# The reciprocal behind the mask: signed factors on the sums of a nested attention kernel

## The chip, the cores and the metric

The kernel runs on one core of a Trainium2 chip. The metric is the time of one execution on the device, in microseconds. The engines' names are those of the profile: PE is the tensor engine (PEld its weight loads), DVE the vector engine, ACT the scalar engine, POOL GpSimd, SP the engine that issues the DMAs.

## What is computed

Self-attention over 32 sequences of different lengths (between 64 and 511 rows of 512 numbers), with 8 heads of 64 and one weight matrix for queries, keys and values. Rows behind a sequence's end are zero in the output.

```python
for b in range(batch):
    x_b = x[b, :lengths[b]]
    q, k, v = np.split(np.matmul(x_b, w_qkv), 3, axis=-1)      # then split into heads
    scores = scale * np.matmul(q, k.transpose(0, 2, 1))
    attn = np.exp(scores - scores_max)
    attn = attn / (np.sum(attn, axis=-1, keepdims=True) + 1e-08)
    output[b, :lengths[b]] = np.matmul(attn, v)                # heads side by side
```

## The kernel before

The kernel first sorts the sequences by length on the chip, longest first, and then works on them in pairs: one round of a loop is two sequences, called the first and the second position (j is 0 and 1). There are twelve loops, one for each width in `LOOPS` (512, 448, then 384 down to 96 in steps of 32); a sequence of N rows is n tiles of 128 rows. For these lengths the rounds are: 512 one, 448 one, 384 one, 352 three, 320 one, 288 one, 256 one, 224 two, 192, 160, 128 and 96 one each. Loops of 4 tiles are 512 and 448; of 3 tiles 384 to 288; of 2 tiles 256 to 160; of 1 tile 128 and 96.

While the scores, exponentials and value products of one sequence run, PE also makes queries, keys and values of the next: its order within a position is written out by hand in `ORDER` (L238), step by step, with the PSUM banks of each step. "S" are scores, "A" value products, "B" queries and keys, "U" values there; "P" makes the next mask on DVE and lets POOL cast the next input; "X" transposes it by DMA; "L" writes the live rows' ones. What is ready for whom is kept by counting semaphores that `plan_waits` (L41) derives: an operation waits for the last writer or reader of each bank and tile it needs. A wait compares a semaphore with a register that grows from round to round.

The values tile `v_aug` has 65 columns a head: 64 values, and one column that is 1 for live keys and 0 for dead ones. So the value product over a bank gives, for each head and query tile, 64 sums and in column 64 (`HD`) the sum of the weights. Three DVE operations then make the output of a bank's heads, one set for each bank (`normed`, L1701) or for two neighbouring banks (`both_normed`, L1663):

- R (L1706, L1671): reciprocal of column 64, from PSUM into a small tile `rcp` of 4, 6 or 8 numbers a row.
- U (L1712, L1680): `rcp` times the ones and zeros of the live query rows, so that dead rows come out as zero. These are read from column 64 of `v_aug`, or, in the loops whose last tile is at most half full ("shared": 448, 320, 288, 192, 160), from a small tile `queries`, which `live_queries` (L1169) fills.
- O (L1715, L1693): the 64 sums of each head times `rcp`, from PSUM into the output tile `out_nat`. When O is done, PE may write the bank again, and SP may store the tile.

The loops of one tile have forms of their own (L1725 for a single bank), which fold the live rows into O.

Ahead of the loops stand the sort, the first casts and transposes and the whole projection of the first sequence. Each semaphore is given a start, its lead (L1905 on): the greatest distance, in positions, over which anyone waits for it. At L2048 these leads are put on by the owning engine (those of DVE by SP) before its first work. The list of operations of that head, in order, is `before_loops` (L382).

Of the kernel before, what the change touches and what calls it, by code (L numbers as in the profile page):

```python
# [18 lines left out]
P = 128  # L19
# [5 lines left out]
class Op:  # L25
# [12 lines left out]
    passed: object = None  # L38


def plan_waits(head, bodies, entries, rare):  # L41
# [22 lines left out]
    def follow(chain):  # L64
# [5 lines left out]
        for at, v in enumerate(chain):  # L70
# [10 lines left out]
            for w, j, k, op in todo:  # L81
# [17 lines left out]
                for wait in waits[w, j, k]:  # L99
                    got = [  # L100
                        o
                        for o in seen[wait[1]]
                        if wait[0] in ("last", "entry", "head", "lead")
                        or (wait[0] == "pos" and o["b"] == b - wait[2])
                        or (wait[0] == "iter" and o["b"] // 2 == b // 2 - wait[2])
                        or (wait[0] == "posin" and o["b"] == first - wait[2])
                        or (wait[0] == "posold" and older and o["b"] == first - wait[2])
                        or (wait[0] == "iterin" and o["b"] // 2 == first // 2 - wait[2])
                    ]
                    if got:  # L110
                        learn(got[-1])
# [7 lines left out]
                for o in sorted(needs, key=lambda o: -o["order"]):  # L119
# [23 lines left out]
                    else:  # L143
                        wait = ("pos", o["name"], b - o["b"])
# [8 lines left out]
                after = dict(mine)  # L153
# [9 lines left out]
                for r in op.writes:  # L163
                    write[r] = o
                    readers[r] = []
# [11 lines left out]
def kernel(  # L177
# [25 lines left out]
    def ring(n, shape, dtype, name, pool=const):  # L203
# [178 lines left out]
    def before_loops():  # L382
# [505 lines left out]
        )  # L888
        computed = small(
# [138 lines left out]
    def position(N, j, at, ring):  # L1028
# [140 lines left out]
        def live_queries():  # L1169
# [3 lines left out]
                scalar1=0.0,  # L1173
                scalar2=None,
                op0=ALU.add,
# [360 lines left out]
        def used_by(blocks, late=False):  # L1536
            if packed:
                mine = [todo.index(block) for block in blocks]
                mine = {min(k, len(todo) - 1) // across for b in mine for k in (b, b + 1)}
# [59 lines left out]
        def paired(p):  # L1599
# [7 lines left out]
                banks[k][:, 0 : heads * n * (HD + 1)].rearrange("p (g t d) -> p g t d", t=n, d=HD + 1)  # L1607
# [54 lines left out]

        def both_normed(both, ks):  # L1663

            k0, k1 = ks
            apart = both[1] - both[0]
            sums_ = psum[:, k0 : k1 + 1, 0 : heads * n * (HD + 1)]
            r = r_bufs[k0][:, 0 : 2 * heads * n]

            def reciprocal():  # L1670
                return nc.vector.reciprocal(  # L1671
                    out=r.rearrange("p (z g) -> p z g", z=2),
                    in_=sums_.rearrange("p z (g d) -> p z g d", d=HD + 1)[:, :, :, HD],
                )

            def only_live():
                rows = queries[:, 1 - j, 0:n] if half_last else v_aug[:, 0:n, both[0], HD]
                rows = rows.unsqueeze(1).broadcast_to([P, 2 * heads, n])
                each = r.rearrange("p (g t) -> p g t", t=n)
                return nc.vector.tensor_tensor(out=each, in0=each, in1=rows, op=ALU.mult)  # L1680

            def divide():
                to = o_t[:, 0:n, :].rearrange("p t (h d) -> p h t d", d=HD)
                if heads == 1:
                    to = to[:, both[0] : both[1] + 1 : apart]
                    got = sums_.rearrange("p z (t d) -> p z t d", d=HD + 1)[:, :, :, 0:HD]
                    by = r.rearrange("p (z t) -> p z t", t=n).unsqueeze(3).broadcast_to([P, 2, n, HD])
                else:
                    to = to[:, both[0] : both[1] + heads].rearrange("p (z g) t d -> p z g t d", z=2)
# [477 lines left out]
```

## Time and profile before

| | |
|---|---|
| median of 3 runs | 329.05 us (328.48 to 329.23) |
| profiled execution: first to last instruction | 328.5 us; the page has no other time of it |
| mean granted clock of PE | 0.994 |
| DMA | 68.85 MB, mean 210 GB/s |
| DVE waiting for PE, largest group (L1367) | 44.8 us in 39 waits |
| POOL waiting for DVE's masks (L1052) | 174.9 us in 28 waits |

A line of a group names the source line, the engine, the operation, the tiles as out<-in, the shapes as partitions x elements with their types, and the count; then busy us, mean ns of one, and the idle time of the engine ahead of them with what ended it. A row of the timeline gives the start and length in us; a stretch of equal instructions is one row, and square brackets hold the idle time before it. The chain is followed back from the last instruction to what released each step.

### The profile page before, as it was taken

Reading aid. Unit: us, or ns where it says so; the run is one execution under the profiler, and the core shown is the slowest. Engines: PE = TensorE matmul, PEld = TensorE weight load, DVE = VectorE, ACT = ScalarE, POOL = GpSimd, SP = SyncE. Lnnn points to the kernel's source line nnn. Section 1 sums busy time; section 2 is a strip of 40 time slices with the busy share of each in tenths; the row PEclk is TensorE's granted clock in tenths of the full one; section 3 lists DMA queues with packets and bytes.
Section 4 is the critical chain, followed back from the end, with each engine's and each line's share of the span. In section 5 each row is a group of like instructions: output and inputs, shape, how many; then the busy total and the mean of one; then the engine's idle time right before and its main releaser. Section 6 shows DMA issues by size and latency. Waiting matters only on the chain.

```text
span 328.5 us, 13310 instructions
## 1 busy us (share of the span) xinstructions
PE 311.6 (95%) x5092; PEld 202.3 (62%) x5092; DVE 197.7 (60%) x635; ACT 262.6 (80%) x413; POOL 101.9 (31%) x148
## 2 busy tenths in 40 slices
PE   6899999999999999999999999999998999999980
PEld 4444645555655556556656657667777886777860
DVE  6777567566666646456455465545575565776853
ACT  4379999897878988988978989899867779687761
POOL 6448040324030330330231243043222224435320
PEclk9999999999999999999999999999999999999997
DMA  6984749395858999696676766857459857966651
GB/s 217 382 278 80 251 140 327 76 354 153 304 52 298 224 269 258 197 268 224 233 214 224 255 194 205 211 174 242 156 131 227 183 176 164 223 206 177 193 180 66
DMA packets 69449, 68.85 MB, mean 210 GB/s; under 512 B 40720, under 2 KB 40720, under 8 KB 69392
## 3 DMA queue, kind: packets, MB, share of 16 engines
q1 hardware_dynamic: 69344, 68.12, 71.4%
q8 instruction: 33, 0.54, 0.7%
q14 instruction: 24, 0.20, 0.2%
q10 hardware_dynamic: 48, 0.00, 0.0%
HBM read 25.17 MB, written 33.55 MB: 179 GB/s over the span
## 4 chain that ended last, share of the span: by engine, by line
PE 84%; DVE 5%; DMA 3%; issue 2%; ACT 2%; SPq 1%; POOL 1%; DVEq 0%; POOLq 0%; ACTq 0%
PE banks L1323 41%; PE banks L1269 13%; PE banks L1517 12%; PE banks L300 6%; PE banks L311 6%; PE banks L1631 2%; DMA xT<-x 2%; DMA x_nat<-in_x_dram 2%; PE banks L1210 1%; PE banks L1557 1%; DVE out_nat L1715 1%; DVE rcp L1712 1%; DVE out_nat L1693 1%; SPq L328 1%; ACT et L1287 1%
## 5 line engine op out<-in xcount | busy, mean ns | idle before, releaser
L1287 ACT ACTIVATE et<-banks 128x704 f16<-128x704 f32 (+8 forms) x256 | 198.8, 825 | 27.8 <-PE banks L1269 24.7
L371 POOL TENSOR_TENSOR x<-x_nat,mask 128x512 f16<-128x512 f32 x83 | 84.2, 1041 | 184.3 <-DVE mask L1052 174.9
L1323 PE MATMUL banks<-xT,w_r 64*128 64x352 f16 (+9 forms) x1536 | 127.8, 294 | 1.8 <-DMA xT<-x 1.2
L1323 PEld LDWEIGHTS banks<-xT,w_r 64*128 64x128 f16 x1536 | 68.7, 94 | 39.0 <-PE banks L1323 8.5
L1269 PE MATMUL banks<-qz,kT 64*128 64x352 f16 (+11 forms) x624 | 77.5, 294 | 2.6 <-issue 0.7
L1715 DVE TENSOR_TENSOR out_nat<-banks,rcp 128x256 f32<-128x256 f32 (+1 forms) x110 | 53.0, 482 | 3.8
L1367 DVE CAST qz<-banks 128x448 f16<-128x448 f32 (+6 forms) x47 | 26.4, 561 | 45.2 <-PE banks L1323 44.8
L1517 PEld LDWEIGHTS banks<-v_aug,et 128*128 128x128 f16 x1240 | 41.7, 97 | 13.5 <-issue 6.8
L1517 PE MATMUL banks<-v_aug,et 128*128 128x65 f16 x1240 | 47.1, 194 | 0.0
L1323 PE MATMUL banks<-w_r,xT 64*128 64x512 f16 (+1 forms) x368 | 46.6, 372 | 0.3 <-ACT v_aug L1489 0.3
L1269 PEld LDWEIGHTS banks<-qz,kT 64*128 64x128 f16 x624 | 28.1, 93 | 25.9 <-issue 7.1
L1706 DVE RECIPROCAL rcp<-banks 128x4 f32<-128x4 f32 (+1 forms) x112 | 20.3, 181 | 20.7 <-PE banks L1517 7.3
L311 PE MATMUL banks<-w_r,xT 128*128 128x512 f16 x104 | 26.9, 381 | 0.5 <-DVE xT L782 0.5
L1386 DVE CAST v_aug<-banks 128x512 f16<-128x512 f32 x25 | 16.6, 690 | 17.9 <-PE banks L1323 17.9
L1323 PEld LDWEIGHTS banks<-w_r,xT 64*128 64x128 f16 x368 | 17.2, 94 | 14.1 <-PE banks L1323 1.0
L1367 ACT CAST kT<-banks 128x352 f16<-128x352 f32 (+6 forms) x47 | 22.5, 479 | 1.5 <-PE banks L1323 1.5
L300 PE MATMUL banks<-xT,w_r 128*128 128x160 f16 (+3 forms) x256 | 23.0, 243 | 0.5 <-DVE v_aug L1489 0.5
L1367 DVE CAST kT<-banks 128x352 f16<-128x352 f32 (+5 forms) x33 | 17.9, 552 | 7.7 <-PE banks L1323 7.6
L300 PEld LDWEIGHTS banks<-xT,w_r 128*128 128x128 f16 x256 | 16.6, 98 | 5.2 <-DMA xT<-x 0.6
L1367 ACT CAST qz<-banks 128x352 f16<-128x352 f32 (+6 forms) x33 | 15.3, 465 | 3.7 <-PE banks L1323 3.6
L1489 ACT CAST v_aug<-banks 128x512 f16<-128x512 f32 x15 | 8.8, 589 | 9.5 <-PE banks L311 9.5
L1631 PE MATMUL banks<-v_aug,et 64*128 64x65 f16 x624 | 14.2, 190 | 0.6 <-issue 0.6
(116 smaller groups left out, 193.3 us busy)
## 6 DMA issues: line engine op xcount, KB each, us to landing
x_nat<-in_x_dram SPq DMA_DIRECT2D x12, 768.0 KB, 6.4
out_dram<-out_nat SPq DMA_DIRECT2D x12, 768.0 KB, 4.0
x_nat<-in_x_dram SPq DMA_DIRECT2D x14, 512.0 KB, 4.5
out_dram<-zeros SPq DMA_DIRECT2D x12, 512.0 KB, 3.6
out_dram<-out_nat SPq DMA_DIRECT2D x12, 512.0 KB, 4.7
out_dram<-out_nat SPq DMA_DIRECT2D x4, 1024.0 KB, 7.0
x_nat<-in_x_dram SPq DMA_DIRECT2D x3, 1024.0 KB, 5.3
out_dram<-zeros SPq DMA_DIRECT2D x4, 768.0 KB, 4.7
```

Of the source, the lines that this page charges most:

```text
L300: last = nc.tensor.matmul(dst[:, 0:N], w_r[:, c, w0 : w0 + P], xT[:, c, 0:N], start=(c == 0), stop=(c == NC - 1),)
L311: last = nc.tensor.matmul(pv, xT[:, c, t * P : (t + 1) * P], w_r[:, c, 2 * D : 3 * D], start=(c == 0), stop=(c == NC - 1),)
L371: return engine.tensor_tensor(out=x16, in0=x32, in1=live.broadcast_to([P, D]), op=ALU.mult)
L1269: last = nc.tensor.matmul(psc[par][:, x * wide : x * wide + N], kT[r, i, c0 : c0 + P], qz[r, i, 0:N], start=True, stop=True,)
L1287: return nc.scalar.activation(out=et[:, :, x0:x1, 0:N], in_=got.rearrange("p j (x q) -> p j x q", q=wide)[:, :, x0:x1, 0:N], func=AF.Exp, ...
L1323: last = nc.tensor.matmul(to, lhs(rows, c), rhs(rows, c), start=(c == 0 and opens), stop=(c == NC - 1 and not opens),)
L1367: return lambda copy, bank: copy(out=buf[:, ms, 0:M], in_=bank[:, 0 : gm * M].rearrange("p (m q) -> p m q", q=M),)
L1386: return lambda copy, bank: copy(out=v_bufs[o][:, t, :, 0:HD], in_=bank.rearrange("p (h d) -> p h d", d=HD))
L1517: last = nc.tensor.matmul(pav[:, g, qt, :], e_bufs[e][:, c0 + qt * P : c0 + (qt + 1) * P], v_aug[:, kt, h, :], start=(kt == 0 and not (hal ...
L1631: last = nc.tensor.matmul(pavs[own][:, g, qt, :], e_bufs[e][rows, c0 + qt * P : c0 + (qt + 1) * P], (v_bufs[0] if ending else v_aug)[rows, ...
L1706: return nc.vector.reciprocal(out=rcp, in_=pav[:, :, :, HD])
L1715: return nc.vector.tensor_tensor(out=o_t[:, 0:n, h0 * HD : (h0 + heads) * HD].rearrange("p t (g d) -> p g t d", d=HD), in0=pav[:, :, :, 0:HD],
```

## The change

In the loops of 2 to 4 tiles the live query rows become factors of +1 (live) and -1 (dead). U now comes first: it multiplies the sums in column 64, read from PSUM, by these factors, into `rcp`. R then takes the reciprocal of `rcp` in place. O is max(rcp, 0) times the 64 sums, as one SCALAR_TENSOR_TENSOR: a dead row's negative reciprocal becomes 0. `queries` now holds the factors in all these loops: a new operation in the head fills it for the first sequence, and step "L" of the second position refills it where it did not before. A bank's sums lie by query tile and then head ("t g d") instead of head and then tile. O over two neighbouring banks is two instructions, one for each bank. The three copies into `queries` at the entries of the loops 448, 320 and 192 go.

The diff also brings in hooks whose tables are empty (`BACKS`, `LATE`), rewraps the text of `ORDER` without changing a step, and sets the leads of all operations that aren't DMAs or among five rare ones to one common number.

```diff
+        op(
+            "queries",
+            "DVE",
+            lambda: dve.tensor_scalar(
+                out=queries[:, 1, :], in0=alive[:, 0, :], scalar1=2.0, scalar2=-1.0, op0=ALU.mult, op1=ALU.add
+            ),
...
                 in0=alive[:, bass.ds(at("DVE") + j, 2), 0:n],
-                scalar1=0.0,
-                scalar2=None,
-                op0=ALU.add,
+                scalar1=2.0,
+                scalar2=-1.0,
+                op0=ALU.mult,
+                op1=ALU.add,
...
             pav = banks[k][:, 0 : heads * n * (HD + 1)].rearrange(
-                "p (g t d) -> p g t d", t=n, d=HD + 1
+                "p (t g d) -> p g t d", t=n, d=HD + 1
...
+        def parted(h0, sums_, r):
+
+            by = r.rearrange("p (t g) -> p t g", t=n).unsqueeze(3).broadcast_to([P, n, heads, HD])
+            return nc.vector.scalar_tensor_tensor(
+                out=o_t[:, 0:n, h0 * HD : (h0 + heads) * HD].rearrange("p t (g d) -> p t g d", d=HD),
+                in0=by,
+                scalar=0.0,
+                in1=sums_.rearrange("p (t g d) -> p t g d", t=n, d=HD + 1)[:, :, :, 0:HD],
+                op0=ALU.max,
+                op1=ALU.mult,
+            )
...
             def divide():
+                if n > 1:
+                    for z in range(2):
+                        last = parted(both[z], sums_[:, z], each[:, z])
+                    return last
...
             def reciprocal():
-                return nc.vector.reciprocal(out=rcp, in_=pav[:, :, :, HD])
+                return nc.vector.reciprocal(out=r, in_=total if n == 1 else r)
 
             def only_live():
-                rows = v_aug[:, 0:n, h0 : h0 + heads, HD].rearrange("p t g -> p g t")
-                if half_last:
-                    rows = queries[:, 1 - j, 0:n].unsqueeze(1).broadcast_to([P, heads, n])
-                return nc.vector.tensor_tensor(out=rcp, in0=rcp, in1=rows, op=ALU.mult)
...
+                rows = queries[:, 1 - j, 0:n].unsqueeze(2).broadcast_to([P, n, heads])
                 return nc.vector.tensor_tensor(
...
+                    out=r.rearrange("p (t g) -> p t g", t=n),
+                    in0=total.rearrange("p (t g) -> p t g", t=n),
+                    in1=rows,
                     op=ALU.mult,
                 )
...
-            whose = f"queries{j}" if half_last else f"vl{j}"
-            op(f"U{h0}", "DVE", only_live, (f"r{k}", whose), (f"r{k}",))
-            op(f"O{h0}", "DVE", divide, (f"bk{k}", f"r{k}"), (f"o{j}.{h0}",))
+            op(f"U{h0}", "DVE", only_live, (f"bk{k}", f"queries{j}"), (f"r{k}",))
+            op(f"R{h0}", "DVE", reciprocal, (f"r{k}",), (f"r{k}",))
+            op(f"O{h0}", "DVE", lambda: parted(h0, sums_, r), (f"bk{k}", f"r{k}"), (f"o{j}.{h0}",))
...
+            elif kind == "L" and not half_last and j:
+                op(
+                    "L",
+                    "DVE",
+                    lambda: (live_queries(), live(alive, 0, n))[1],
+                    (),
+                    (f"vl{o}", "queries0", "queries1"),
+                )
...
-                nc.vector.tensor_copy(out=queries[:, 1, 0:n], in_=v_bufs[0][:, 0:n, 0, HD])
...
+    alike = [name for name in lead if name not in by_dma | rare and lead[name]]
+    for name in alike:
+        lead[name] = max(lead[k] for k in alike)
```

Three places on DVE, with buffer numbers and waits. The first is the first position of loop 512, where the banks of the last two heads' products (`a7` and `a6`, on PE) are turned into output; `rcp_88` is the small tile of bank 3, `out_nat_77` the output tile. Before:

```order
L1706 RECIPROCAL rcp_88<-banks 128x4 [waits done_a7]
L1712 TENSOR_TENSOR rcp_88<-rcp_88,v_aug_67 128x4 [waits done_R7]
L1715 TENSOR_TENSOR out_nat_77<-banks,rcp_88 128x4x64 [waits done_ST0,done_U7]
L1706 RECIPROCAL rcp_87<-banks 128x4 [waits done_a6]
L1712 TENSOR_TENSOR rcp_87<-rcp_87,v_aug_67 128x4 [waits done_R6]
L1715 TENSOR_TENSOR out_nat_77<-banks,rcp_87 128x4x64 [waits done_U6]
```

With the change, at the same place:

```order
L1748 TENSOR_TENSOR rcp_88<-banks,queries 128x4 [waits done_a7]
L1744 RECIPROCAL rcp_88<-rcp_88 128x4 [waits done_U7]
L1682 SCALAR_TENSOR_TENSOR out_nat_77<-rcp_88,banks 128x4x64 [waits done_ST0,done_R7]
L1748 TENSOR_TENSOR rcp_87<-banks,queries 128x4 [waits done_a6]
L1744 RECIPROCAL rcp_87<-rcp_87 128x4 [waits done_U6]
L1682 SCALAR_TENSOR_TENSOR out_nat_77<-rcp_87,banks 128x4x64 [waits done_R6]
```

The product has moved ahead of the reciprocal and reads the bank and `queries`; the reciprocal has the small tile on both sides; the waits stand at the same places.

The second is the first position of loop 224, two banks at once. Before:

```order
L1671 RECIPROCAL rcp_85<-banks 128x8 [waits done_a1]
L1680 TENSOR_TENSOR rcp_85<-rcp_85,v_aug_67 128x8 [waits done_R1]
L1693 TENSOR_TENSOR out_nat_77<-banks,rcp_85 128x4x2x64 [waits done_ST0,done_U1]
L1671 RECIPROCAL rcp_91<-banks 128x8 [waits done_a0]
L1680 TENSOR_TENSOR rcp_91<-rcp_91,v_aug_67 128x8 [waits done_R0]
L1693 TENSOR_TENSOR out_nat_77<-banks,rcp_91 128x4x2x64 [waits done_U0]
```

With the change:

```order
L1709 TENSOR_TENSOR rcp_85<-banks,queries 128x8 [waits done_a1]
L1700 RECIPROCAL rcp_85<-rcp_85 128x8 [waits done_U1]
L1682 SCALAR_TENSOR_TENSOR out_nat_77<-rcp_85,banks 128x2x128 [waits done_ST0,done_R1]
L1682 SCALAR_TENSOR_TENSOR out_nat_77<-rcp_85,banks 128x2x128
L1709 TENSOR_TENSOR rcp_91<-banks,queries 128x8 [waits done_a0]
L1700 RECIPROCAL rcp_91<-rcp_91 128x8 [waits done_U0]
L1682 SCALAR_TENSOR_TENSOR out_nat_77<-rcp_91,banks 128x2x128 [waits done_R0]
L1682 SCALAR_TENSOR_TENSOR out_nat_77<-rcp_91,banks 128x2x128
```

Each O of 512 elements has become two of 256.

The third is the start of the second position of loop 352, with the change (before, the first of these rows is not there):

```order
L1185 TENSOR_SCALAR queries<-alive 128x2x3
L1164 ISA
L1164 TENSOR_SCALAR v_aug_67<-alive 128x24
L1067 ISA [waits done_C]
L1067 TENSOR_SCALAR mask_79<-alive 128x4
```

One instruction has come in ahead of the live rows and the mask. The rows of PE, ACT, POOL and SP are the same as before in what they do, in their order and in the semaphores that they wait for; only the increments ahead of the first work differ (PE 9 for 1, ACT 7 for 0, SP 14 for 8).

More of the change, by code (lines that the diff above doesn't have):

```diff
@@ L104, in follow @@
                         or (wait[0] == "pos" and o["b"] == b - wait[2])
+                        or (wait[0] == "back" and at > chain.index(v) and o["b"] == b - wait[2])
                         or (wait[0] == "iter" and o["b"] // 2 == b // 2 - wait[2])
@@ L143, in follow @@
                     else:
[L144 removed]
+                        wait = ("back" if op.eng in BACKS and b - o["b"] > (j or 0) else "pos", o["name"], b - o["b"])
                     alike = [u for u in waits[w, j, k] if len(wait) > 2 and u[:2] == wait[:2]]
@@ L1900 @@
     waits, has = plan_waits(head, bodies, entries, rare)
+    for todo in waits.values():
+        for wait in [w for w in todo if w[0] == "back"]:
+            for other in [w for w in todo if w[0] in ("posin", "posold") and w[1] == wait[1]][:1]:
+                todo.remove(other)
+                todo[todo.index(wait)] = (*wait, other[0], other[2])
     def op_of(v, j, k):
@@ L1911 @@
                 continue
-            least = wait[2] if len(wait) > 2 else wait[0] in ("last", "lead")
+            least = max(wait[2::2]) if len(wait) > 2 else wait[0] in ("last", "lead")
             lead[wait[1]] = max(lead[wait[1]], least)
@@ L1941, in value_of @@
             return "pos", lead[name] + 1 - wait[2] + j
+        if wait[0] == "back":
+            entering = wait[3:] and (wait[3], lead[name] + 1 - wait[4])
+            return "back", (lead[name] + 1 - wait[2] + j, *entering)
         if wait[0] == "iter":
@@ L2100, with backs_of, late @@
                 nc.sync.reg_sub(here["until"], of(ends[last], "SP"), 2)
-            body, after = f"loop_{N}", f"after_{N}"
-            nc.br_lt(pair, ends[v], on_true=body, on_false=after)
+            body, after, again, rest = f"loop_{N}", f"after_{N}", f"again_{N}", f"rest_{N}"
+            only_pe = [nc.tensor.engine]
+            def backs_of(e):
+                for key in sorted(backs[v, e]):
+                    EN[e].reg_mul(regs[e][key], of(pair, e), 2)
+                    EN[e].reg_add(regs[e][key], regs[e][key], key[1][0])
+            def late():
+                for k in tails_of[v]:
+                    issue(v, 1, k, bodies[v][1][k], late=True)
+            rotated = bool(tails_of[v])
+            early = rotated and v + 1 < len(LOOPS) and apart(v + 1)
+            nc.br_lt(pair, ends[v], on_true=body, on_false=f"past_{N}" if early else after)
             with nc.body(body):
@@ L2123 @@
                             eng.reg_add(reg, reg, raised[base])
+                    if e != "PE" or not rotated:
+                        backs_of(e)
                 for e, eng in EN.items():
-                    back = eng.br_lt(pair, ends[v], on_true=body, on_false=after)
+                    if e == "PE" and rotated:
+                        eng.br_lt(pair, ends[v], on_true=again, on_false=rest)
+                        continue
+                    back = eng.br_lt(pair, ends[v], on_true=body, on_false=again if rotated else after)
                     if e in hints:
                         back.branch_hint(hints[e])
+            if rotated:
+                with nc.body(again):
+                    late()
+                    backs_of("PE")
+                    nc.br(body, engines=only_pe)
+                if early:
+                    with nc.body(f"past_{N}"):
+                        enter(v + 1, "PE")
+                        nc.br(after, engines=only_pe)
+                with nc.body(rest):
+                    if early:
+                        enter(v + 1, "PE")
+                    late()
             nc.switch_bb(after)
```

140 lines of the change are left out of this document (90 added, 50 removed), and 63 rows, old and new, of the table ORDER.

## The prediction

> **What bounds the kernel now.** I read the page's busy shares and chain first, then who waits for the normalisation's last operation, then the forms on VectorE (DVE).
>
> ```profile
> span 328.5 us, 13310 instructions
> PE 311.6 (95%) x5092; PEld 202.3 (62%) x5092; DVE 197.7 (60%) x635; ACT 262.6 (80%) x413; POOL 101.9 (31%) x148
> ...
> PE 84%; DVE 5%; DMA 3%; issue 2%; ACT 2%; SPq 1%; POOL 1%; DVEq 0%; POOLq 0%; ACTq 0%
> ```
>
> TensorE (PE) is busy for 95% of the span and holds 84% of the chain that ended last; DVE has 5% of the chain and sits idle for 40% of the span. So time saved on DVE counts only where PE stands still behind DVE. The change touches operations R, U and O; O frees the PSUM bank, so PE waits for O alone. Its lines (L1715, and L1693 for two banks at once) name the waiters, each with us and times (L1715's first, L1693's below the dots):
>
> ```profile
> L1715 DVE TENSOR_TENSOR out_nat<-banks,rcp x110: 423/425/559, 29.4 to 311.2; 128x256 f32<-128x256 f32 x62, 128x384 f32<-128x384 f32 x48
>   PEld banks L1269: 2.1, 7
>   PEld banks L1517: 0.7, 2
>   PE banks L1269: 0.4, 2
>   PE banks L1323: 0.2, 1
> ...
>   PEld banks L1269: 0.5, 1
>   PE banks L1269: 0.4, 1
> ```
>
> Weight loads (PEld) waited 10 times for 2.1 + 0.7 + 0.5 = 3.3 us, but the matmul stream itself stood still only 4 times, for 0.4 + 0.2 + 0.4 = 1.0 us. That 1.0 us is all that a faster DVE chain can give directly.
>
> **The chain R, U, O, reordered.** The groups on DVE, with mean ns of one behind the busy us:
>
> ```profile
> L1715 DVE TENSOR_TENSOR out_nat<-banks,rcp 128x384 f32<-128x384 f32 x48 | 26.7, 557 | 1.6
> L1715 DVE TENSOR_TENSOR out_nat<-banks,rcp 128x256 f32<-128x256 f32 x62 | 26.3, 424 | 2.1
> ...
> L1706 DVE RECIPROCAL rcp<-banks 128x4 f32<-128x4 f32 x64 | 11.2, 175 | 8.6 <-PE banks L1557 5.5 <-PE banks L1517 1.9 <-PE banks L1631 1.0
> L1706 DVE RECIPROCAL rcp<-banks 128x6 f32<-128x6 f32 x48 | 9.1, 190 | 12.1 <-PE banks L1631 5.5 <-PE banks L1517 5.3 <-PE banks L1557 0.6
> ...
> L1725 DVE SCALAR_TENSOR_TENSOR out_nat<-banks,real,rcp 128x256 f32<-128x256 f32 x2 | 1.0, 484 | 0.1
> ...
> L540 DVE TENSOR_SCALAR h_hit_i<-h_idx_f,h_rank,h_idc_f 32x32 f16<-32x32 f32 x1 | 0.3, 289 | 0.0
> ...
> L523 DVE TENSOR_SCALAR h_cmp<-h_key_row,h_key_col 32x32 f32<-32x32 f32 x1 | 0.2, 228 | 0.0
> ...
> L841 DVE SCALAR_TENSOR_TENSOR h_four<-h_later,h_own 128x16 f32<-128x16 f32 x1 | 0.2, 174 | 0.0
> ```
>
> *U on PSUM.* No small product over PSUM was traced. The two O forms give (557 - 424)/128 = 1.04 ns an element, so 4 elements over PSUM come to 424 - 252 x 1.04 = 162 ns; U on SBUF takes 161 to 169 ns when nothing disturbs it (rows below). No difference.
>
> *R on SBUF.* Not traced. Over PSUM it is 175 ns at 4 and 190 ns at 6 elements. Since a product shows no difference between the two sources, I take the same; as bounds, 15 ns less and 15 ns more.
>
> *O as SCALAR_TENSOR_TENSOR.* The one form over PSUM, L1725, takes 484 ns where the product takes 424. But its scalar is a column (`real`), and going from one such column to two (h_cmp to h_hit_i) costs 289 - 228 = 61 ns by itself. The added form has a constant. With a constant, on SBUF, h_four takes 174 ns at 16 elements; the product U, 161 at 4, comes at 1.04 ns an element to 173 at 16. So I take 424 and 557 ns, unchanged; bounds 0 and +60 ns (PSUM stands as the second operand now, which no row shows).
>
> The chain of one group is thus the same length, R + U + O, and no wait is added: U waits where R did.
>
> **What the new order takes away.** U before reads two SBUF tiles. Its durations, min/median/max:
>
> ```profile
> L1712 DVE TENSOR_TENSOR rcp<-rcp,v_aug x56: 164/169/693, 28.7 to 275.6; 128x6 f32<-128x6 f32 x32, 128x4 f32<-128x4 f32 x24
> L1712 DVE TENSOR_TENSOR rcp<-rcp,queries x54: 161/164/916, 69.9 to 311.0; 128x4 f32<-128x4 f32 x38, 128x6 f32<-128x6 f32 x16
> ```
>
> Half of all stay at 169 ns or below, and the longest takes 916. The timeline there shows why:
>
> ```profile
> 277.63 2.04 POOL L371 TENSOR_TENSOR x<-x_nat,mask 128x512 f16<-128x512 f32 x2 [4.10 <-DVE mask L1052]
> ...
> 278.35 1.48 PE L1323 MATMUL banks<-xT,w_r 64*128 64x192 f16 x32
> ...
> 278.77 0.92 DVE L1712 TENSOR_TENSOR rcp<-rcp,queries 128x4 f32<-128x4 f32 x1
> ...
> 281.09 0.11 PEld L1269 LDWEIGHTS banks<-qz,kT 64*128 64x128 f16 x4 [0.27 <-DVE out_nat L1715]
> 281.09 0.34 PE L1269 MATMUL banks<-qz,kT 64*128 64x192 f16 x4
> ```
>
> U ends at 278.77 + 0.92 = 279.69, as GpSimd's (POOL's) casts end at 277.63 + 2.04 = 279.67. O, with one operand in SBUF and one in PSUM, never exceeds 559 ns in 110 runs. The new U has O's kind of operands, so I expect its stretches to go. The Trainium skill's page "SBUF — State Buffer", section "Who interferes with whom", says the same: two SBUF inputs on the Vector engine collide with GpSimd's reads, one does not. The trace agrees (916 against 559 ns).
>
> But PE had matmuls to run meanwhile (1.48 us from 278.35): the 0.75 us stretch ended in a weight-load wait of 0.27 us, and the matmul row at 281.09 has no idle time. Bounds: 0 (no matmul idle time marked) to the 1.0 us that matmuls ever stood behind O. I take **-0.15 us**, half the weight-load wait, near the end that the matmul row shows.
>
> **What it adds.** *Split O.* Nine two-bank O of 512 elements become two of 256: two in the loop 256, three in each of the two rounds of 224, one in 192. The pipelined starts decide:
>
> ```profile
> 286.78 0.69 DVE L1693 TENSOR_TENSOR out_nat<-banks,rcp 128x512 f32<-128x512 f32 x1
> 287.39 0.17 DVE L1706 RECIPROCAL rcp<-banks 128x4 f32<-128x4 f32 x1
> ...
> 287.79 0.42 DVE L1715 TENSOR_TENSOR out_nat<-banks,rcp 128x256 f32<-128x256 f32 x1
> 288.13 0.17 DVE L1706 RECIPROCAL rcp<-banks 128x4 f32<-128x4 f32 x1
> ```
>
> After a 512 O the next starts 0.61 us later, after a 256 O 0.34 us later: 2 x 0.34 - 0.61 = 0.07 us each. PE waits behind such an O once (0.4 us above): **+0.07 us**, bounds 0 and 9 x 0.07 = 0.6.
>
> *One TENSOR_SCALAR on `queries`* at the second position in the loops 512, 384, 352 (three rounds), 256 and 224 (two): 8 of them.
>
> ```profile
> 282.91 0.16 DVE L1170 TENSOR_SCALAR queries<-alive 128x4 f16 x1
> 282.97 0.18 DVE L1179 TENSOR_SCALAR v_aug<-lasts 128x8 f16 x1
> ```
>
> The next starts 0.06 us later. Behind it on DVE stands the mask, for which POOL's cast waits, and behind that the transposes. **+0.05 us**, bounds 0 and 8 x 0.06 = 0.5. Three copies of as few elements go, at the entries of the loops 448, 320 and 192; at 0.06 us each that is 0.2 at most, and I count nothing.
>
> *The head.* The uniform leads add semaphore increments ahead of the first work: PE 1 to 9, ACT 0 to 7, SP 8 to 14. First the rows of the increments' line, then of the timeline, last of the chain:
>
> ```profile
> L2051 SPq EVENT_SEMAPHORE  x8: 17/17/17, 2.4 to 2.8; - x8
> ...
> L2051 PEldq EVENT_SEMAPHORE  x1: 51/51/51, 1.0 to 1.0; - x1
> ...
> 1.93 2.74 PE L457 MATMUL banks<-h_ones 128*128 128x256 f16 x12 [1.93 <-POOL h_ones L447]
> ...
> 7.55 0.64 DVE L366 TENSOR_SCALAR x<-x_nat,mask 128x512 f16<-128x512 f32 x1 [0.51 <-DMA x_nat<-in_x_dram]
> ...
> 12.62 0.40 PE L773 MATMUL banks<-h_ident,x 128*128 128x128 f16 x4 [0.27 <-POOL x L371]
> ...
> 5.90 5.55 DMA x_nat<-in_x_dram
> ```
>
> SP's eight stand 0.06 us apart, 3.5 times their length; on PE eight more cost 8 x 51 ns = 0.4 to 3.5 times that, 1.4 us; I take 1.1. PE's twelve warming matmuls, which end at 1.93 + 2.74 = 4.67, the sort's matmuls behind them and the masks that DVE makes from the sort then come 1.1 us later. The wait for x_nat absorbs 0.51, the idle time at 12.62 another 0.27, POOL's cast path (the transfer landing at 11.45) is not touched by PE. SP's six cost 0.36 us, of which up to that much could delay the transfer at 5.90. That leaves 1.1 - 0.51 - 0.27 = 0.3 at most by way of PE; I take **+0.2 us** in all, bounds 0 and 0.3 + 0.36 = 0.7.
>
> **Sum**: 328.5 - 0.15 + 0.07 + 0.05 + 0.2 = 328.7 on the profiled span. The page gives no time beside its span; the median shown, 329.05, is 0.55 above it, so the forecast is **329.2 us**: no change that can be told.
>
> **Rivals.**
>
> *The stretches are worth more.* If nearly all of the 1.0 us went with the stretches (-0.9) and the head cost nothing (0 for 0.2), the sum would be 328.5 - 0.9 + 0.12 = 327.7, or **328.2 us** by the median. For it: 916 ns is several times U's usual length, and what follows on DVE slides with it. Against: PE's matmul row behind that stretch shows no idle time.
>
> *O is slower in the new form.* From +60 ns an O (the L1725 price) PE pays at its 10 weight-load waits and 4 matmul waits: 14 x 0.06 = 0.8 us: **330.0 us, slower**. It decides from about 35 ns an O (14 x 0.035 + 0.17 = 0.66). Against: the constant-scalar rows.
>
> *PE starts late and gets its full pace late.* The same warming matmul, by stretch:
>
> ```profile
> L457 PE MATMUL banks<-h_ones 128*128 128x384 f16 x2 | 0.8, 512 | 0.0
> ...
> L457 PE MATMUL banks<-h_ones 128*128 128x384 f16 x5 | 1.1, 363 | 0.0
> ```
>
> Before 6.7 us it takes 512 ns, after 6.8 us 363: the pace rises 4.9 us after the first matmul. With a first matmul at 3.0 that becomes 7.9, still ahead of the first real work, 12.62 and the transposes before it. Should it rise some 2 us later still, V's matmuls up to 12.62 take twice as long, and about 1 us passes the 0.27 us of idle time: **330.2 us, slower**. The Trainium skill's "TensorE: Matmul & The Clock Gate", section "Part 1: The HAM clock gate", says the busy window of some 3.4 us runs freely, so that the rise may miss a window; one trace cannot show that.
>
> *The change doesn't do what it says:* R, now SBUF to SBUF, takes over the stretches. A one-source operation can be held too:
>
> ```profile
> 23.19 0.93 DVE L1149 TENSOR_SCALAR v_aug<-alive 128x32 f16 x1
> ```
>
> Then -0.15 falls away: **329.4 us**. The Trainium skill's section on who interferes with whom lists copy, cast and tensor_scalar among the operations that can be held, as this row shows, and doesn't name the reciprocal.
>
> **Chances.** Forecast 0.48; stretches worth more 0.22; slower O 0.13; late pace 0.12; R takes the stretches 0.05. A measurement of this kernel tells 0.2% (0.66 us) from no change. Faster 0.22; within 0.2% 0.48 + 0.05 = 0.53; slower 0.25. The range runs from the first rival, 328.2, to the slower ones, 330.2.
>
> **What would show it.** Right: U never above 200 ns, R near 175 and 190, O near 424 and 557, PE's first matmul near 3.0 us, its waits on out_nat in the loops as before. Wrong: O at 484 (the slower O), R with stretches up to 0.9 us (the last rival), 512 ns matmuls beyond 8.2 us (the late pace), or the waits of 1.0 us gone and the span under 328.

## The result, and the profile after

| | before | changed |
|---|---|---|
| median of 6 runs each | 328.65 us (327.58 to 329.23) | 331.56 us (330.14 to 334.57) |
| ratio | | 1.0115, 95% interval 1.0082 to 1.0147 |
| first to last instruction, profiled execution | 328.5 us | 328.2 us (this execution took 330.14 us) |

The changed kernel is slower by about 1.15% by the ratio (the two medians of the table lie 2.9 us, or 0.9%, apart), and its 331.56 us lie outside the range of the prediction. Its profiled execution is the shortest of the six; the spans of the others go up to 332.6 us. So the page after looks almost like the page before, and most of the loss has to be looked for elsewhere. First what came as predicted. The page's head, busy shares and chain of the changed kernel:

```profile
span 328.2 us, 13348 instructions
PE 310.4 (95%) x5092; PEld 201.4 (61%) x5092; DVE 194.4 (59%) x650; ACT 263.0 (80%) x413; POOL 102.2 (31%) x148
...
PE 88%; DVE 3%; issue 2%; ACT 2%; DMA 1%; SPq 1%; POOL 0%; ACTq 0%; POOLq 0%; DVEq 0%
```

DVE is busy 3.3 us less (197.7 before) and has 3% of the chain against 5%. The changed kernel's rows by source line for U (L1748, L1709), R (L1744) and O (L1682): minimum, median and maximum in ns, then for O who waited for it.

```profile
L1748 DVE TENSOR_TENSOR rcp<-banks,queries x110: 151/157/166, 28.4 to 309.3; 128x4 f32<-128x4 f32 x62, 128x6 f32<-128x6 f32 x48
...
L1744 DVE RECIPROCAL rcp<-rcp x110: 177/179/193, 28.6 to 309.5; 128x4 f32<-128x4 f32 x62, 128x6 f32<-128x6 f32 x48
...
L1709 DVE TENSOR_TENSOR rcp<-banks,queries x9: 156/166/167, 239.8 to 284.9; 128x8 f32<-128x8 f32 x9
...
L1682 DVE SCALAR_TENSOR_TENSOR out_nat<-rcp,banks x128: 412/422/555, 28.8 to 309.7; 128x256 f32<-128x256 f32 x80, 128x384 f32<-128x384 f32 x48
...
  PEld banks L1285: 1.7, 5
  PE banks L1285: 0.4, 2
  PEld banks L1533: 0.3, 1
  PEld banks L317: 0.2, 1
  PE banks L1339: 0.2, 1
  PEld banks L306: 0.2, 1
```

U never takes more than 167 ns (916 before), R in place has no stretch, O is as long as it was. Weight loads wait 1.7 + 0.3 + 0.2 + 0.2 = 2.4 us for O (3.3 before), matmuls 0.4 + 0.2 = 0.6 us (1.0 before).

Then the head of the changed kernel. First, by source line, the increments of the uniform leads, then PE's timeline (start, length, instruction, idle time before it):

```profile
L2115 SPq EVENT_SEMAPHORE  x14: 17/17/17, 2.4 to 3.2; - x14
L2115 PEldq EVENT_SEMAPHORE  x9: 51/51/51, 1.0 to 2.3; - x9
L2115 ACTq EVENT_SEMAPHORE  x7: 17/17/17, 1.3 to 1.8; - x7
```

```profile
3.06 2.72 PE L463 MATMUL banks<-h_ones 128*128 128x256 f16 x12 [3.06 <-POOL order_i L494]
...
8.50 0.40 PE L779 MATMUL banks<-h_ident,x 128*128 128x128 f16 x4 [0.71 <-DVE x L372]
```

PE's first matmul comes at 3.06 us instead of 1.93: the nine increments stand about 0.16 us apart, three times their length. The first transposes of x begin at 8.50.

What nothing in the prediction spoke of stands at the start of the loop 192. PE's timeline of the changed kernel there, then two rows by source line: the branch into the loop (L2197) and the waits on semaphores that follow it (L2094), with first and last start.

```profile
272.78 0.66 PE L1533 MATMUL banks<-v_aug,et 128*128 128x65 f16 x16
274.65 0.51 PE L1285 MATMUL banks<-qz,kT 64*128 64x192 f16 x8 [1.21 <-ACT v_aug L1402]
```

```profile
L2197 PEldq COMPARE_BRANCH  x1: 68/68/68, 273.3 to 273.3; - x1
...
L2094 PEldq EVENT_SEMAPHORE  x4: 51/51/51, 274.4 to 274.8; - x4
```

The same place in the kernel before:

```profile
274.20 0.66 PE L1517 MATMUL banks<-v_aug,et 128*128 128x65 f16 x16
275.09 0.51 PE L1269 MATMUL banks<-qz,kT 64*128 64x192 f16 x8 [0.23 <-issue]
```

PE stands still for 1.21 us, before for 0.23. The releaser that the profile names is ScalarE's cast, but PE's own sequencer says otherwise: its branch starts at 273.3 and lasts 68 ns, and its next instruction, the first wait, is recorded only at 274.4, 1.09 us behind the branch's end. That gap alone doesn't prove a stall, because a wait's record can start only when the wait is over: in the kernel before, PE's wait for the transposes at 254.4 us starts 0.03 us after they have landed. The semaphores decide. The first wait at the loop 192 is for an operation O, whose semaphore rose at 268.86 us, long before the branch, and again only at 274.81, after the wait. The cast that the profile names was done at 273.97, also before 274.4. So for 1.09 us behind the branch PE issued nothing and waited for nothing that the trace shows. At the start of the loop 128 the same happens, 0.65 us behind the branch at 308.43; the two semaphores of its first wait had risen at 305.27 and 306.59. Changed, then before:

```profile
309.36 0.40 PE L1285 MATMUL banks<-qz,kT 64*128 64x128 f16 x8 [0.81 <-ACT v_aug L1505]
```

```profile
310.10 0.40 PE L1269 MATMUL banks<-qz,kT 64*128 64x128 f16 x8 [0.25 <-ACT v_aug L1489]
```

Both loops are entered with the same instructions as before. PE doesn't jump there either: in the listing of the program the loop's code stands right behind the branch, and the branch lasts 68 ns, as most of those with which PE leaves a loop (67 to 80), while its four branches back to a loop's start last 214 (the loop 160 has one of these: it runs two rounds in the traces, not one). Only the place of PE's code has moved: nine PE instructions more stand ahead of it, eight increments and a register's move.

### The profile page after: what moved, and what is told of

Read it like the earlier page. It is cut to its first block, busy times and chain, and to the rows that moved or that the text cites. A ratio compares the mean times of both kernels' runs of the same rounds, so it can differ in the third digit from the quotient of the medians.

```text
span 328.2 us, 13348 instructions
## 1 busy us (share of the span) xinstructions
PE 310.4 (95%) x5092; PEld 201.4 (61%) x5092; DVE 194.4 (59%) x650; ACT 263.0 (80%) x413; POOL 102.2 (31%) x148
## 4 chain that ended last, share of the span: by engine, by line
PE 88%; DVE 3%; issue 2%; ACT 2%; DMA 1%; SPq 1%; POOL 0%; ACTq 0%; POOLq 0%; DVEq 0%
PE banks L1339 44%; PE banks L1285 14%; PE banks L1533 12%; PE banks L317 7%; PE banks L306 5%; PE banks L1647 3%; PE banks L1226 1%; PE banks L1573 1%; DMA xT<-x 1%; PE banks L463 1%; DVE out_nat L1682 1%; ACT et L1303 1%; PE banks L779 0%; ACT v_aug L1402 0%; SPq L334 0%
## 5 line engine op out<-in xcount | busy, mean ns | idle before, releaser
L1682 DVE SCALAR_TENSOR_TENSOR out_nat<-rcp,banks 128x256 f32<-128x256 f32 (+1 forms) x128 | 59.5, 470 | 5.2 <-DMA out_dram<-out_nat 1.0
L1748 DVE TENSOR_TENSOR rcp<-banks,queries 128x4 f32<-128x4 f32 (+1 forms) x110 | 17.5, 159 | 21.2 <-PE banks L1647 7.5
L1744 DVE RECIPROCAL rcp<-rcp 128x4 f32<-128x4 f32 (+1 forms) x110 | 20.2, 184 | 3.8
```

Of the source, the lines that this page charges most:

```text
L1682: return nc.vector.scalar_tensor_tensor(out=o_t[:, 0:n, h0 * HD : (h0 + heads) * HD].rearrange("p t (g d) -> p t g d", d=HD), in0=by, scal ...
L1744: return nc.vector.reciprocal(out=r, in_=total if n == 1 else r)
L1748: return nc.vector.tensor_tensor(out=r.rearrange("p (t g) -> p t g", t=n), in0=total.rearrange("p (t g) -> p t g", t=n), in1=rows, op=ALU. ...
```

## The experiments

Ratios are against the kernel before on the same chip, with 95% intervals.

### Which part of the change costs?

`e1`: the changed kernel without the uniform leads.

```diff
-    by_dma = {op.name for body in bodies for ops in body for op in ops if op.dma}
-    alike = [name for name in lead if name not in by_dma | rare and lead[name]]
-    for name in alike:
-        lead[name] = max(lead[k] for k in alike)
```

> The changed kernel without the four lines that make the leads uniform (alike); the new order R, U, O on VectorE, the split O and the operations on queries stay. Instructions ahead of the first work are then as before. Theory A (the loss comes from the head, where PE's first matmul moved from 1.93 to 3.06 us): 328.3 to 328.9, no time over the kernel before, spans near 328 and first matmul at 1.9. Theory B (the loss comes from the new VectorE code in the loops): 331 to 332, with spans up to 332 as in the changed kernel. Theory C (part lies in the about 2 us of the changed kernel outside first to last instruction, and these come with the leads): the difference of time and span falls back to under 1 us.

Measured: 327.64 against 328.26 us, ratio 0.9986 (0.9970 to 1.0002). The whole loss is gone, so it came with these four lines, and theory B falls. Theory C falls as well: time less span is 1.8 us in this kernel and in the kernel before, about 2.0 in five of the six runs of the changed one (3.4 in the sixth).

`e2`: the same four lines added to the kernel before.

> The kernel before with only the four lines of the uniform leads added: PE issues 9 increments ahead of its first matmul for 1, ScalarE 7 for 0, SyncE 14 for 8, and the registers that go with them. Theory A (head): about 331.5, spans from 328 to 332 and a granted clock down to 0.988 in the long ones, first matmul near 3.0 us. Theory B (VectorE code in the loops): 328.7 as before. Theory C: about 2 us between time and span.

Measured: 331.75 us, ratio 1.0093 (1.0071 to 1.0115). The leads alone make the loss.

`e3`: the kernel before with eight increments on PE.

```diff
+        for _ in range(8):
+            nc.tensor.sem_inc(passed, 1)
         pair = nc.alloc_registers("pair")
```

> The kernel before with eight more semaphore increments on PE alone ahead of its first matmul, on a semaphore that nobody waits for. If PE's late first matmul is the whole of the loss: about 331.5. If ScalarE's, SyncE's or the registers' part counts as well: between 328.7 and 331. If the loss is not in the head: 328.7.

Measured: 331.50 us, ratio 1.0104 (1.0082 to 1.0126). PE's eight increments are enough; ScalarE's, SyncE's and the registers add nothing that can be told.

`e4`: the changed kernel, with PE's increments moved behind its warming matmuls.

```diff
-            if amount and name in owner:
+            if amount and name in owner and owner[name] != "PE":
...
+            if op.name == "warm1b":
+                for name, amount in lead.items():
+                    amount -= name in ahead
+                    if amount and owner.get(name) == "PE":
+                        nc.tensor.sem_inc(sems[name], unit(name) * amount)
```

> The changed kernel with PE's eight increments of the uniform leads put behind its three runs of warming matmuls; ScalarE's and SyncE's stay ahead. First matmul back near 2.0 us. If PE's late first matmul is the whole of the loss: 328.3 to 328.9. If ScalarE's and SyncE's increments cost too: 329 to 331. If the loss is not in the head: 331.5.

Measured: 331.14 us, ratio 1.0079 (1.0057 to 1.0101), although the first matmul is back at 1.93 us. Theory A, by which PE's late start is the loss, falls. PE's matmul number 200 comes only 0.33 us later than in `e1`, its last one 3.7 us later. Comparing the branches of all kernels so far gave theory D: the two stalls stand in the changed kernel, `e2`, `e3` and `e4`, and not in the kernel before and `e1`.

### Is it where PE's code stands?

`e5`: the kernel before, with eight PE instructions inside a branch of the loop 256 that isn't taken for these lengths. Nothing more is executed; the code behind moves. (`e8` has 4 in place of the 8.)

```diff
         with begin:
             for k, op in ops:
                 issue(v, j, k, op)
+            if e == "PE" and skip < 0 and LOOPS[v] == 256 and any(op.name in sems for _, op in ops):
+                for _ in range(8):
+                    nc.tensor.sem_inc(passed, 1)
```

> The kernel before with eight more semaphore increments on PE inside a branch of the loop 256 that is never taken on this data: nothing more is executed, but all of PE's code from the loop 224 on stands eight instructions further on. Theory D (where PE's code stands decides: in the four kernels with more PE instructions the branch into the loop 192 was followed by 1.09 to 1.17 us without an instruction, the branch into the loop 128 by 0.65 us, against 0.06 us in the kernel before and in the one without uniform leads): both stalls appear, 1.04 + 0.60 = 1.6 us, so 329.7 to 330.5. Theory A (the head alone): 328.3, no stalls.

Measured: 331.37 against 328.22 us, ratio 1.0087 (1.0058 to 1.0116): nearly the whole loss, and more than the 1.6 us that theory D gave. The rows by source line of the branch (L2105) and the waits behind it (L2033) in `e5`, then its timeline at the loop 192:

```profile
L2105 PEldq COMPARE_BRANCH  x1: 68/68/68, 274.5 to 274.5; - x1
...
L2033 PEldq EVENT_SEMAPHORE  x4: 51/51/51, 275.7 to 276.0; - x4
```

```profile
275.90 0.51 PE L1269 MATMUL banks<-qz,kT 64*128 64x192 f16 x8 [1.29 <-ACT v_aug L1386]
```

The stall is there without one executed instruction more: 274.5 to 275.7.

`e6`: the changed kernel with 64 such instructions at the same place.

> The changed kernel, with 64 increments on PE in the same never-taken branch of the loop 256, so that PE's code from the loop 224 on stands 64 instructions further on; the uniform leads stay in the head. Counted in PE instructions, the first of the loop 192 stands then at 8 past a multiple of 256 (200 in the changed kernel, 191 before), that of the loop 128 at 4 (196; 187). Theory D, with places of 192 and more as the dear ones: both stalls go, 328.5 to 330 with the head's part left over. Theory A: 331.5 as in the changed kernel.

Measured: 328.74 us, ratio 1.0011 (0.9994 to 1.0027). The uniform leads and their increments are all still executed. Its timeline at the loop 192:

```profile
273.50 0.51 PE L1285 MATMUL banks<-qz,kT 64*128 64x192 f16 x8 [0.18 <-issue]
```

`e7`: `e3` with 64 such instructions, which leaves the eight executed increments in the head and takes the stalls away.

> The kernel before with eight more PE increments ahead of its first matmul (as in the run with PE increments alone, 331.5) and 64 never-executed ones in the loop 256, which by theory D takes the stalls away again: what is left is the head's part. Theory D: 328.8 to 329.6 (the head's 0.3 to 1.1 us) and no stalls. Theory A: 331.5.

Measured: 329.15 us, ratio 1.0028 (1.0012 to 1.0043), about 0.9 us, and no stalls. That isn't purely the head: the 64 instructions are there too, and `e12` below, which has them without the late start, is at 1.0008.

`e8`: four instead of eight.

> The kernel before with four never-executed PE instructions in the loop 256: the loop 192 then begins at 195 past a multiple of 256, the loop 128 at 191. If theory D holds and the border is at 192: the 1.04 us stall at the loop 192 appears, none at the loop 128, 329.2 to 329.6. If the border lies above 195: neither, 328.3. If any shift does it: both, 330.

Measured: 328.52 us, ratio 1.0016 (0.9994 to 1.0037), no stalls. Not any shift does it.

### Which places are dear?

> The kernel before with the eight never-executed PE instructions in the loop 192's never-taken branch: the loop 192 begins where it did (191 past a multiple of 256), the loop 128 eight further on (195, as in the shift-alone run, where it stalled). If the place of the branch's own target decides: the stall of 0.60 us at the loop 128 alone, none at the loop 192, 328.6 to 329.2 and a good part of the 3.1 us of the shift-alone run gone. If what decides is code of the loop 224 shifting, or anything executed before: no stall, 328.2.

`e9` has the eight in the loop 192 (`LOOPS[v] == 192`). Measured: 328.71 us, ratio 1.0010 (0.9990 to 1.0030), no stall at either loop, though the loop 128 stands where it stalled in `e5`. So its own place alone doesn't decide.

> The kernel before with six never-executed PE instructions in the loop 256: the loop 192 begins at 197 past a multiple of 256, between 195 (no stall with a shift of four) and 199 (stall with eight); the loop 128 at 193, between 191 (none) and 195 (stall). If the border for the loop 192 is 196: its stall of 1.04 us appears, about 329.3 to 330.5; if it lies between 198 and 199: none, 328.4. Nothing in the runs so far says which of the two; the loop 128 likewise.

`e10` (`range(6)` in the loop 256). Measured: 328.29 us, ratio 1.0001 (0.9976 to 1.0025), no stalls. Between a shift of six and one of eight lie 3 us.

> The changed kernel without the uniform leads once more, against the kernel before: is it faster by more than can be told? Before: 327.64 against 328.26, ratio 0.9986 (0.9970 to 1.0002). If VectorE's new order is worth the 0.15 us less 0.12 us of the prediction: 328.2. If it is worth what the first comparison shows: 327.6, ratio 0.998 with an interval that ends under 1.

`e11` is `e1` once more. Measured: 328.42 against 328.19 us, ratio 1.0014 (0.9991 to 1.0037). It doesn't repeat the gain of `e1`: the new order on VectorE is worth nothing that can be told.

> The changed kernel with the uniform leads kept but both of their costs taken away: PE's eight increments behind its warming matmuls (331.1 by itself) and PE's code from the loop 224 on moved 64 instructions further on (328.74 by itself). If head and code place are the two causes and add up: 327.7 to 328.5, no stall at the loops 192 and 128. If a third cause hides in the leads (ScalarE's or SyncE's increments, the registers): about 328.7 as with the code moved alone, or more.

`e12` is `e4` with the 64 of `e6`. Measured: 328.48 us, ratio 1.0008 (0.9995 to 1.0021): the change with all its leads, and no loss that can be told.

> The kernel before with 24 never-executed PE instructions in the loop 256: the loop 192 begins at 215 past a multiple of 256, the loop 128 at 211. Theory E (from about 198 on to the next multiple of 256 every place is dear, since the code that the loop needs crosses that multiple early): the stall of about 1.1 us at the loop 192, 330 to 331.5. Theory F (only a narrow place near 199 and 200 is dear): no stalls, 328.2.

`e13` (`range(24)`). Measured: 330.01 us, ratio 1.0052 (1.0037 to 1.0068). No stall at the loop 192, one of 0.60 us at the loop 128.

> The kernel before with 48 never-executed PE instructions in the loop 256: the loop 192 begins at 239 past a multiple of 256, the loop 128 at 235. Theory E: the stall at the loop 192, 330 to 331.5. Theory F: no stalls, 328.2. A stall at 215 and none at 239 would be a band that ends between them.

`e14` (`range(48)`). Measured: 328.76 us, ratio 1.0014 (0.9999 to 1.0030), no stall. Neither theory E nor theory F holds with these two.

> The kernel before with eight never-executed PE instructions in the loop 256 (alone: 331.37, stalls at the loops 192 and 128) and 128 more in the loop 192's never-taken branch: the loop 192 begins at 199 as there, the loop 160 at 214, the loop 128 at 67 for 195. At 195 the loop 128 stalled behind a stalled loop 192 and did not behind an unstalled one. If its own place is needed too: the stall at the loop 192 alone, 0.6 us less than 331.37. If the second stall only follows from the first: both again, 331.4. If the loop 160 at 214 is dear now: a stall there that no run had.

`e15` (`{256: 8, 192: 128}.get(LOOPS[v], 0)`). Measured: 332.29 us, ratio 1.0123 (1.0068 to 1.0178). The stall at the loop 192 is there, the one at the loop 128 gone. Within the loop 192 the branch over the 128 lasts 1.03 us (0.22 in `e5`), and over 2 us behind it, in the middle of a run of matmuls, stands a new stall, which by the listing is 200 past a multiple of 256. PE passes that place in other blocks of 256 without one.

```profile
286.81 0.39 PE L1323 MATMUL banks<-w_r,xT 64*128 64x256 f16 x4
288.43 0.39 PE L1323 MATMUL banks<-w_r,xT 64*128 64x256 f16 x4 [1.23 <-issue]
```

All kernels together. The places are counted in PE instructions of the program's listing, past a multiple of 256; the stalls are the time between the end of the branch into the loop and PE's next instruction, from the traces, one profiled execution each.

| kernel | place of loop 192, 128 | stall at 192, 128 (us) | ratio |
|---|---|---|---|
| before; `e1`, `e11` | 191, 187 | 0.06, 0.06 | 1; 0.9986, 1.0014 |
| `e9` | 191, 195 | 0.06, 0.06 | 1.0010 |
| `e8` | 195, 191 | 0.06, 0.06 | 1.0016 |
| `e10` | 197, 193 | 0.06, 0.06 | 1.0001 |
| `e3`; `e5` | 199, 195 | 1.17, 0.66; 1.16, 0.66 | 1.0104; 1.0087 |
| changed; `e2`; `e4` | 200, 196 | 1.09, 0.66; 1.09, 0.66; 1.10, 0.65 | 1.0115; 1.0093; 1.0079 |
| `e15` | 199, 67 | 1.17, 0.06 | 1.0123 |
| `e13` | 215, 211 | 0.06, 0.60 | 1.0052 |
| `e14` | 239, 235 | 0.06, 0.06 | 1.0014 |
| `e6`, `e12`; `e7` | 8, 4; 7, 3 | 0.06, 0.06 | 1.0011, 1.0008; 1.0028 |

## Why the prediction was wrong

*The stretches of U (-0.15).* Right in mechanism: they went, R did not take them over, and waits for O fell by 0.9 us on weight loads. The 0.4 us less on matmuls need not be the change's: `e9`, with the old order, has 0.6 us as well. As a whole the VectorE part (`e1`, `e11`) can't be told from no change, as the sum of these steps (-0.15 + 0.07 + 0.05) said; the size of each by itself was not measured.

*O in the new form.* Right: 422 ns for 256 elements, 554 for 384. The rival of a slower O falls.

*The head (+0.2, bounds 0 and 0.7).* PE's first matmul came at 3.06 us as forecast. What this costs was not measured sharply. `e6`, `e7` and `e12` all have the 64 instructions and no stalls; by their ratios the late start costs 0.1 us (`e6` less `e12`) or 0.65 us (`e7` less `e12`), each give or take some 0.7. So nothing shows the term to lie outside its bounds. Single executions say less: matmul 200 comes 0.67 us later than in `e1` in the changed kernel and 1.12 in `e2`, but also 0.76 in the kernel before and 1.09 in `e14`, whose first matmuls come at 1.93. They differ in part because of PE's pace, which rises where the matmuls of 384 columns get short. Groups by form on PE, first of the changed kernel, then of `e2`, whose first matmul also came at 3.07:

```profile
L463 PE MATMUL banks<-h_ones 128*128 128x384 f16 x6 | 1.1, 326 | 0.0
```

```profile
L457 PE MATMUL banks<-h_ones 128*128 128x384 f16 x6 | 2.1, 518 | 0.0
```

In the one all six ran at the full pace, in the other none did; the granted clock rose at 6.1 and 9.05 us. After a first matmul at 1.93 it rose between 3.3 us (`e13`) and 5.95 us (`e10`) later, after one at about 3.0 between 2.98 us (`e3`) and 5.98 us (`e2`) later. So the delay varies by up to 3.0 us, whether PE starts early or late. The Trainium skill's "TensorE: Matmul & The Clock Gate", section "Part 1: The HAM clock gate", describes a window that runs freely; the spread of 3.0 us fits the window of some 3.4 us given there, while the shortest delays, 2.98 and 3.06 us (`e3` and the changed kernel), are less than one whole window. The rival that started from here gave 1 us to a rise some 2 us later; between the changed kernel and `e2` the rise differs by 2.9 us and matmul 200 by 0.45. Its time, 330.2, was nearest to the result, but not for its reason.

*The step that failed* is the way the increments were priced at all: "on PE eight more cost 8 x 51 ns = 0.4 to 3.5 times that, 1.4 us", in the head and nowhere else. That PE's rows are the same in what they do and in their order was taken to mean that the loops cost PE the same time. But eight instructions also move all the code behind them, and the sum has no term for that. It costs about 3 us without being executed (`e5`, 2.9 by its ratio), against 0.1 to 0.65 for the head. This is shown by `e5` (shift alone), `e6` (the loss taken away by a further shift, the increments kept) and `e4` (the loss still there with the first matmul back at 1.93). No row of the profile before holds it: there PE goes on 0.06 us after each of these branches.

*The base.* "The median shown, 329.05, is 0.55 above it" compares two different executions. In the later runs of the kernel before, time less span is 1.8 us (328.61 and 326.8 in one of them). By that the profiled execution with its span of 328.5 us took an estimated 330.3 and was a long one: it holds a wait of 1.24 us for the transposed x at 254.48 us, which `e1` and `e8` don't have. As the forecast was put back on the median of the runs, this cost it little; but terms taken from that execution's waits were taken from one that isn't typical.

*What stays open.* The two stalls add 1.03 + 0.59 = 1.6 of the 3 us. Matmul by matmul the changed kernel's profile falls behind that of `e1` by 0.7 us up to matmul 200, 1.0 at the loop 192, 0.6 at the loop 128 and 0.7 at the last transposes, with 0.2 regained in between. In the profiles of `e2` to `e5` PE also waits 0.7 to 1.6 us for transposes at 253 to 254 us, ahead of the stalls, as it did in the profiled execution of before, and `e10`'s profile loses 0.9 us there without stalls. In six runs of the kernels that stall at the loop 128 the time outside the span is 2.4 to 3.4 us; in no run of the others is it above 2.0.

The last transposes are a part of the loss that comes with the moved code but not with the stalls. In all kernels that stall, and also in `e6`, `e7`, `e12` and `e14`, PE waits 0.7 to 1.4 us for them; the timeline of `e7`:

```profile
316.42 1.53 PE L300 MATMUL banks<-xT,w_r 128*128 128x96 f16 x32 [1.10 <-DMA xT<-x]
```

In these eleven kernels the transposes land 3.5 to 4.3 us after the start of their issue, in the other six (before, `e1`, `e8` to `e11`) 2.4 us after it. The traces hold one more difference: in all eleven a packet of 16 KiB on the queue that loads instructions, by its 33 or 34 packets PE's, starts between issue and landing, and in the six none does, but for one that starts just as they land (`e1`). So moving PE's code seems also to move the moment at which its next block is loaded, and where that falls on the transposes they are late. That the one delays the other was not tried by itself.

And the rule of the dear places wasn't found: 199 and 200 stall at the loop 192, 197 and 215 don't; the loop 128 stalls at 195 in `e5` and not in `e9`. Nor do such stalls need a branch or moved code: in the kernel before PE stands still for 0.63 us at 285.70 in the middle of a run of matmuls, and the profile names no cause.

## What to carry to other kernels

An instruction costs where it is executed and also by moving what stands behind it: if a change leaves an engine's work alone but adds or takes a few instructions ahead of its loops, compare the time from each branch to the engine's next instruction, kernel against kernel, before blaming what was changed on purpose. A gap there is a stall only if the semaphores that the next instruction waits for had risen earlier. Never-executed instructions in a branch that isn't taken move code and cost nothing else that these runs show (`e8`, `e10`), so they tell the two apart in one run. They are also a cheap remedy, but how many help has to be tried: 64 took the loss away here, 24 left one stall, 128 brought a new one. A single profiled execution can lie over 1 us above the typical one: put its span against the times of several runs with spans of their own before taking terms from its waits.

## What the runs showed of the hardware

- Behind the branch at the start of a loop PE issued nothing for 1.09 to 1.17 us (loop 192) or 0.60 to 0.66 us (loop 128), or went on after 0.06 us, by the place of the code alone (`e5`, `e8`, `e10`). The Trainium skill's "Runtime: NRT & Kernel Launch", section "Instruction fetch mechanics", says that code comes in blocks of 16 KiB, 256 instructions, and that a taken branch to a target which isn't loaded has to wait for it. The traces agree with the block (33 instruction packets with 0.54 MB on one queue, and 8657 PE instructions in the listing of before, a matmul with its weight load counted as two). That these stalls are such a wait is not shown: PE doesn't jump at these branches (68 ns against 214), and around the stall of the changed kernel, from 273.3 to 274.4 us, no packet of that queue moves, the nearest one ending 17 us before it and the next starting 1.5 us after its end.
- The last DMA transposes landed 2.4 us after the start of their issue in six executions, and 3.5 to 4.3 us after it in the eleven in which a packet of that queue moved meanwhile.
- A semaphore increment of 51 ns took about 0.16 us of PE's time when several stood in a row (nine from 1.0 to 2.3 us), on SyncE 0.06 for 17 ns.
- The reciprocal from SBUF to SBUF was not held up beside GpSimd's casts: 177 to 193 ns in all 110 executions on up to 6 elements, 8 of these beside a cast. Before, ten products of two SBUF tiles at that place ran beside a cast, and six of them took 218 to 916 ns.
